# The last three steps of both S5 recurrences: one product pass and one and three quarters of a GLU pass put ahead of the transposes

## The chip, the cores and the metric

One core of a Trainium2 chip runs the whole program. The core has a matrix engine (PE, with a weight loader of its own, PEld), a vector engine (DVE), a scalar engine (ACT), a general engine (POOL) and a queue for transfers (SP). Each works through its own list of instructions in order, and they wait for one another by semaphores. The metric is the device time of one execution in microseconds (us), the median of three runs.

## The reference

A trunk of four layers over 512 positions of 1024 channels: S5, gated linear attention, differential attention, S5, each followed by a SwiGLU feed-forward layer, with a final norm. The change lies in the two S5 layers:

```python
def s5_mixer(h, lam_re, lam_im, log_dt, b_re, b_im, c_re, c_im, d_skip, w_glu):
    ...
        bu_re = jnp.einsum('bcgh,gph->bcgp', u_c, bb_re)
        ...
        _, _, s_re, s_im = lax.associative_scan(_cdiag_combine, (a_re, a_im, bu_re, bu_im), axis=1)
        ...
        y = jnp.einsum('bcgp,ghp->bcgh', s_re, cr) - jnp.einsum('bcgp,ghp->bcgh', s_im, ci)
        return (s_re[:, -1], s_im[:, -1]), y
    ...
    y = y + d_skip.astype(f32) * h.astype(f32)
    z = jax.nn.gelu(y).astype(h.dtype)
    a, b = jnp.split(z @ w_glu, 2, axis=-1)
    return a * jax.nn.sigmoid(b)
```

A bank of complex one-pole recurrences is driven by the input `u`, read out into `y`, passed through a GELU to `z`, and `z` goes through a gated linear unit (GLU) of 1024 x 2048 weights.

## The kernel before

Both S5 layers run `s5_pipe`. The 1024 channels are cut into eight blocks of 128, and a loop of ten steps, `kk` = 0 to 9, keeps several blocks in flight. "Block 5" below is the sixth block, and `glu(5)` its GLU products. What happens to a block:

- `up` (line 1447, PE) transposes its input; `products` (line 1468, PE) multiplies it by the input operators into two PSUM banks `V`;
- `states` (lines 1473 to 1478, DVE) rotates `V`, `scan` (line 1482, DVE) runs the recurrence, `turn` (lines 1491 and 1495, DVE) rotates back into the four parts `prods`;
- `outputs` (lines 1502 and 1504, PE) multiplies input and `prods` by the output operators into the bank `y`, and ACT makes the GELU of it (line 1506) into `z`;
- `turned` (line 1516, PE) transposes `z` in four pieces into the bank `zp`; ACT copies `zp` to `zT` rounded for the matrix engine (line 1517), and `rest` (line 1520, DVE) makes what the rounding left, so that `zT` has a high and a low part;
- `glu` (lines 396 to 398, PE) adds the block's share to four accumulators `acc`, one for each tile of 128 positions, three products of 512 columns each (high times high, high times low, low times high): 12 matmuls for a block.

Weights of the GLU are loaded for two blocks at once, and split by ACT (line 368, high) and DVE (line 376, low) at the start of an even step. Blocks 6 and 7 share a pair, which is split in step 8.

A step issues, in this order on PE: `outputs(kk - 1)`, `up(kk + 2)`, `turned(kk - 1)`, `products(kk + 1)`, `glu(kk - 2)`. In step 8 there are no products left, and `glu(6)` stands ahead of `turned(7)`. The order of all five engines in this loop is the order of the code: it is written out by hand (`hand_all`), and no scheduler moves anything in it.

Around the loop the two layers differ. The first one (about 28 to 156 us of the trace) builds its operators while it runs: in its step 6 the operators of block 7 are transposed (line 1270, PE) and copied by ACT (line 1293) into `inm`, which `products(7)` reads, and the skip-and-decay operator of blocks 6 and 7 goes through DRAM and back (lines 1246 to 1261) before `outputs(6)` can read it. The second one (about 1760 to 1852 us) loads its operators from DRAM, where an earlier part of the program put them (SP, lines 1856 and 1861).

Right behind the loop the same four accumulators are emptied by ACT (line 1904), the other three quarters of the GLU follow on PE, and then the feed-forward layer.

Of the kernel before, what the change touches and what calls it, by code (L numbers as in the profile page):

```python
# [24 lines left out]
NT = SEQ // P  # L25
# [263 lines left out]
class Trunk:  # L289
# [1132 lines left out]
    def s5_pipe(self, L, hu, zT, natural, room, get, before=None, hooks=None, steps=None, left=None):  # L1422
# [19 lines left out]
        def up_first(kk):  # L1442
            ps = self.acc("up")[:].rearrange("p (b m) -> p b m", b=4) if left and kk in (1, 2, 3) else self.tp("up")[:]
            ups[kk] = ps
            for b in range(4):
                g0 = 8 * kk + 2 * b
                nc.tensor.transpose(
                    ps[:, b], hu[:, g0 : g0 + 2].rearrange("p g t c -> p (g t c)"), self.ident[:]
                )

        def up(kk):
            if kk not in ups:
                up_first(kk)
            ps, o = ups[kk], room[kk % 4]
            if left and kk < 4:
                v.tensor_tensor(
                    o.rearrange("p (b m) -> p b m", b=4), ps, left.Rt.unsqueeze(1).broadcast_to([P, 4, P]), op=ALU.mult
                )
            else:
                nc.scalar.copy(o, ps.rearrange("p b m -> p (b m)"))  # L1460

        def products(kk):

            U, inm = room[kk % 4], get(kk, "in")
            V[kk] = [self.sbank("V"), self.sbank("V")]
            for z in range(2):
                for b in range(4):
                    mm(V[kk][z][:, bs(b)], inm[:, z, bs(b)], U[:, bs(b)], start=True, stop=True)  # L1468

        def states(kk):  # L1470

            cs, m = get(kk, "cs"), hold[kk % 2][0]
            v.tensor_tensor(m[:, 0], V[kk][0][:], cs[:, 0], op=ALU.mult)
            v.tensor_tensor(m[:, 3], V[kk][0][:], cs[:, 1], op=ALU.mult)
            v.tensor_tensor(m[:, 1], V[kk][1][:], cs[:, 1], op=ALU.mult)
            v.tensor_tensor(m[:, 2], V[kk][1][:], cs[:, 0], op=ALU.mult)
            v.tensor_tensor(m[:, 0], m[:, 0], m[:, 1], op=ALU.add)
            v.tensor_tensor(m[:, 2], m[:, 2], m[:, 3], op=ALU.subtract)

        def scan(kk, z):  # L1480
            m = hold[kk % 2][0]
            v.tensor_tensor_scan(m[:, 1 + 2 * z], get(kk, "r4"), m[:, 2 * z], 0.0, op0=ALU.mult, op1=ALU.add)

        def turn(kk, k):

            cs = get(kk, "cs")
            m, q = hold[kk % 2]
            sh = lambda x: x.rearrange("p (b m) -> p b m", m=P)[:, :, : P - 1]
            a, b = ((1, 0), (3, 1), (3, 0), (1, 1))[k]
            if k == 1:  # L1490
                v.scalar_tensor_tensor(
                    q[:, k, :, 1:], sh(m[:, a]), -1.0, sh(cs[:, b]), op0=ALU.mult, op1=ALU.mult
                )
            else:
                v.tensor_tensor(q[:, k, :, 1:], sh(m[:, a]), sh(cs[:, b]), op=ALU.mult)

        def outputs(kk):

            U, om, mop, q = room[kk % 4], get(kk, "out"), get(kk, "map"), hold[kk % 2][1]
            yb = self.tp("y")  # L1500
            for b in range(4):
                mm(yb[:, b], U[:, bs(b)], mop[:, bs(b)], start=True, stop=False)
                for j in range(4):
                    mm(yb[:, b], q[:, j, b], om[:, j // 2, bs(b)], start=False, stop=j == 3)  # L1504
            z = room[4 + kk % 2].rearrange("p (t n) -> p t n", t=4)
            nc.scalar.activation(
                z.rearrange("p t (g h) -> p g t h", h=16),
                yb[:].rearrange("p b (g t h) -> p (b g) t h", t=4, h=16), AF.Gelu_apprx_tanh,
            )

        def turned(kk):
            z = room[4 + kk % 2].rearrange("p (t n) -> p t n", t=4)
            zps[kk] = zp = self.tp("zp")[:].rearrange("p a b -> p (a b)")
            order = "p (m t) -> p t m" if natural else "p (t m) -> p t m"
            for t in range(4):
                nc.tensor.transpose(zp.rearrange(order, t=4)[:, t], z[:, t], self.ident[:])
            self.last_turned = nc.scalar.copy(zT[:, 0, kk], zp)

        def rest(kk):
            v.tensor_tensor(zT[:, 1, kk], zps[kk], zT[:, 0, kk].bitcast(F32), op=ALU.subtract)  # L1520

        def glu(kk):
            if not accs:
                accs.extend(self.acc() for _ in range(NT))
            hl = hls[kk // 2]
            for t in range(NT):
                ts = slice(t * P, (t + 1) * P)
                self.mm3(
                    accs[t][:], zT[:, 0, kk, ts], zT[:, 1, kk, ts], hl[:, 0, kk % 2], hl[:, 1, kk % 2],
                    kk == 0, kk == KT - 1,  # L1530
                )

        if hooks:
            hook = lambda name, kk: hooks[name](kk) if name in hooks else None
            late = hooks.get("late", ())
            self.hand_all()
            if left:
                for kk in range(4):
                    up_first(kk)
            before(up, products)  # L1540
            for kk in range(10):
                if kk % 2 == 0 and kk:
                    hls[kk // 2 - 1] = self.high(stage[kk // 2 - 1], 2, 512)
                hook("first", kk)
                if kk < 8:
                    states(kk)
                if kk == 7:
                    rest(5)
                if kk - 1 in late:
                    scan(kk, 0)  # L1550
                    scan(kk, 1)
                    rest(kk - 2)
                if kk % 2 == 0 and kk:
                    self.low(hls[kk // 2 - 1], stage[kk // 2 - 1])
                hook("behind states", kk)
                if 1 <= kk < 9 and kk not in late:
                    outputs(kk - 1)
                hook("operators", kk)
                if kk + 2 < 8:
                    up(kk + 2)  # L1560
                hook("ahead of zp", kk)
                if kk == 8:
                    glu(6)
                if 1 <= kk < 9 and kk not in late:
                    turned(kk - 1)
                if kk + 1 < 8:
                    products(kk + 1)
                hook("behind products", kk)
                if kk < 8:
                    if kk - 1 not in late:  # L1570
                        scan(kk, 0)
                        scan(kk, 1)
                    hook("behind scans", kk)
                    for k in range(4):
                        turn(kk, k)
                hook("beside", kk)
                if kk in late:
                    outputs(kk - 1)
                    turned(kk - 1)
                elif 1 <= kk < 9 and kk != 6:  # L1580
                    rest(kk - 1)
                if kk % 2 == 0 and kk < 8:
                    stage[kk // 2] = self.staged(self.wb_src(wg, kk, D), 2, 512)
                if kk >= 2 and kk != 8:
                    glu(kk - 2)
                hook("last", kk)
            self.hand()
            return accs
# [5 lines left out]
        for kk in range(11):  # L1594
            if kk < 8:
                products(kk)
                states(kk)
            if 1 <= kk < 9:
                scan(kk - 1, 0)
                turn(kk - 1, 0)  # L1600
                scan(kk - 1, 1)
                for k in (1, 2, 3):
                    turn(kk - 1, k)
            if kk + 1 < 8:
                up(kk + 1)
            if steps:
                steps(kk)
            if 2 <= kk < 10:
                outputs(kk - 2)
            if kk % 2 == 0 and kk < 8:  # L1610
                stage[kk // 2] = self.staged(self.wb_src(wg, kk, D), 2, 512)
            if kk % 2 and 3 <= kk:
                j = (kk - 3) // 2
                hls[j] = self.halves(stage[j], 2, 512)
            if 2 <= kk < 10:
                turned(kk - 2)
                rest(kk - 2)
            if kk >= 3:
                glu(kk - 3)
# [944 lines left out]
```

## Time and profile before

| what | us |
|---|---|
| three runs | 2268.05, 2264.08, 2266.39 (median 2266.39) |
| the profiled execution, its own time | 2265.08 |
| its span, first to last instruction | 2263.3 |
| PE busy | 2200.7 |
| DVE busy | 1561.8 |
| ACT busy | 1121.4 |
| mean granted clock of PE | 0.992 |

The profiled execution's own time is 1.78 us above its span and 1.31 us under the median of the runs. A row of a timeline below has the start in us, the duration in us, the engine, the line, the operation, output and inputs, shapes and the number of merged instructions; at its end, in brackets, stands how long the engine was idle before it and who ended that. A matmul of full-precision operands has two entries in the trace (a `products` pass is 16 entries, an `outputs` pass 40), and one of the GLU has one. The end of a matmul is modelled, and the next one starts before it.

### The profile page before, as it was taken

How to read it: one execution, taken by the hardware profiler on the slowest of the kernel's cores; microseconds unless marked ns; L12 is line 12 of the kernel's file. 1: busy time of each engine (PE TensorE's matmuls, PEld its weight loads, DVE VectorE, ACT ScalarE, POOL GpSimd, SP SyncE). 2: the span in 40 equal slices, each digit the busy share in tenths (PEclk: the TensorE clock that was granted, in tenths of full speed). 3: DMA queues.
4: the chain of work that ended last, by engine and by line, in shares of the span. 5: the costliest groups of instructions: out<-in, count | busy, mean ns of one | idle time of the engine just before them, and what ended most of it. 6: DMA issues, size and time to landing. Idle time of an engine off the chain costs nothing.

```text
span 2263.3 us, 37243 instructions
## 1 busy us (share of the span) xinstructions
PE 2200.7 (97%) x14847; PEld 1952.7 (86%) x14847; DVE 1561.8 (69%) x2424; ACT 1121.4 (50%) x1878; POOL 281.2 (12%) x392
## 2 busy tenths in 40 slices
PE   5999999999999999999999999999999899999998
PEld 4878979889777799998988887999998788989997
DVE  9963977776625479777754675977766964967675
ACT  6534645453453456555535676744544224635343
POOL 1000141522000011101002131111000100101000
PEclk8999999999999999999999999999999999999999
DMA  4257475663422557766336366985641546676632
GB/s 88 52 154 188 115 192 159 172 188 90 124 75 65 142 143 185 191 162 172 99 127 142 91 147 161 237 219 134 175 101 39 147 144 166 169 186 158 168 75 75
DMA packets 296039, 317.83 MB, mean 140 GB/s; under 512 B 72285, under 2 KB 235417, under 8 KB 295482
## 3 DMA queue, kind: packets, MB, share of 16 engines
q1 hardware_dynamic: 233626, 234.23, 34.4%
q0 software_dynamic: 62240, 81.22, 19.3%
q8 instruction: 117, 1.92, 0.4%
q14 instruction: 56, 0.46, 0.1%
HBM read 283.54 MB, written 16.65 MB: 133 GB/s over the span
## 4 chain that ended last, share of the span: by engine, by line
PE 83%; DVE 8%; ACT 4%; issue 2%; DMA 1%; SPq 1%; POOL 0%; ACTq 0%; DVEq 0%; POOLq 0%
PE a L541 18%; PE acc L396 14%; PE acc L398 13%; PE acc L397 13%; PE c L541 8%; PE d L541 4%; PE y L1504 2%; DVE whl L376 2%; ACT whl L368 1%; PE V L1468 1%; PE op L2366 1%; PE s L2332 1%; PE tp L123 1%; DVE halves L229 1%; ACT halves L211 1%
## 5 line engine op out<-in xcount | busy, mean ns | idle before, releaser
L376 DVE TENSOR_TENSOR whl<-wst,whl 128x1024 fp32r<-128x1024 f32 x272 | 331.2, 1222 | 260.7 <-ACT whl L368 260.2
L368 ACT CAST whl<-wst 128x1024 fp32r<-128x1024 f32 x272 | 283.9, 1050 | 310.3 <-PE acc L398 227.2
L541 PE MATMUL a<-side,whl 128*128 128x256 f32 x3168 | 382.3, 277 | 4.0 <-DVE whl L376 3.6
L541 PEld LDWEIGHTS a<-side,whl 128*128 128x128 f32 x3168 | 369.0, 188 | 6.8 <-DVE whl L376 5.4
L396 PE MATMUL acc<-whl,act 128*128 128x512 f32 x680 | 268.9, 396 | 1.9 <-DVE x L524 1.9
L397 PE MATMUL acc<-whl,act 128*128 128x512 f32 x680 | 265.3, 390 | 0.0
L398 PE MATMUL acc<-whl,act 128*128 128x512 f32 x680 | 265.3, 390 | 0.0
L541 PE MATMUL c<-side,whl 128*128 128x256 f32 x2112 | 254.3, 277 | 1.2 <-DVE whl L376 1.2
L541 PEld LDWEIGHTS c<-side,whl 128*128 128x128 f32 x2112 | 246.7, 188 | 2.0 <-DVE whl L376 2.0
L376 DVE TENSOR_TENSOR whl<-slot,whl 128x1024 fp32r<-128x1024 f32 x107 | 130.4, 1221 | 70.4 <-ACT whl L368 70.4
L396 PEld LDWEIGHTS acc<-whl,act 128*128 128x128 f32 x680 | 127.6, 188 | 31.3 <-issue 2.7
L368 ACT CAST whl<-slot 128x1024 fp32r<-128x1024 f32 x107 | 112.2, 1053 | 83.0 <-PE acc L398 34.9
L398 PEld LDWEIGHTS acc<-whl,act 128*128 128x128 f32 x680 | 127.7, 188 | 27.0
L397 PEld LDWEIGHTS acc<-whl,act 128*128 128x128 f32 x680 | 127.7, 188 | 24.7
L396 PE MATMUL acc<-whl,hT 128*128 128x512 f32 x352 | 142.6, 405 | 0.0
L398 PE MATMUL acc<-whl,hT 128*128 128x512 f32 x352 | 138.1, 392 | 0.0
L397 PE MATMUL acc<-whl,hT 128*128 128x512 f32 x352 | 137.8, 392 | 0.0
L541 PE MATMUL a<-sides,whl 128*128 128x256 f32 x1056 | 134.5, 283 | 0.0
L541 PEld LDWEIGHTS a<-sides,whl 128*128 128x128 f32 x1056 | 129.7, 191 | 1.2
L541 PE MATMUL d<-sides,whl 128*128 128x256 f32 x1056 | 126.5, 276 | 1.0 <-ACT whl L368 1.0
L541 PEld LDWEIGHTS d<-sides,whl 128*128 128x128 f32 x1056 | 122.8, 188 | 1.2 <-ACT whl L368 1.2
L680 ACT CAST act<-r 128x512 fp32r<-128x512 f32 (+1 forms) x110 | 66.4, 646 | 114.9 <-DVE r L659 107.6
(478 smaller groups left out, 3909.9 us busy)
## 6 DMA issues: line engine op xcount, KB each, us to landing
wst<-in_ffn_w_gate_up_dram SPq DMA_DIRECT2D x88, 512.0 KB, 4.7
wst<-in_ffn_w_down_dram SPq DMA_DIRECT2D x88, 512.0 KB, 4.4
slot<-in_ffn_w_gate_up_dram SPq DMA_DIRECT2D x71, 512.0 KB, 5.3
wst<-in_ffn_w_gate_up_dram POOLq DMA_DIRECT2D x44, 512.0 KB, 6.3
halves<-in_ffn_w_gate_up_dram SPq DMA_DIRECT2D x43, 512.0 KB, 5.4
wst<-in_s_w_glu_dram SPq DMA_DIRECT2D x32, 512.0 KB, 4.7
wst<-in_gla_w_in_dram SPq DMA_DIRECT2D x24, 512.0 KB, 3.7
wst<-in_diff_w_qkv_dram SPq DMA_DIRECT2D x24, 512.0 KB, 4.4
```

Of the source, the lines that this page charges most:

```text
L123: tr.nc.tensor.transpose(p[:, j], h[:, j * P : (j + 1) * P], tr.ident[:])
L211: self.tr.nc.scalar.mul(self.F[t // 2, d][:, j, (t % 2) * P : (t % 2 + 1) * P], p[:, j], self.gcol[:, 4 * d + j : 4 * d + j + 1])
L229: v.tensor_tensor(s, s, y, op=op)
L368: self.last["high"] = self.nc.scalar.copy(hl[:, 0], w[:])
L376: self.last["low"] = self.nc.vector.tensor_tensor(hl[:, 1], w[:], hl[:, 0].bitcast(F32), op=ALU.subtract)
L396: mm(out, lh, rh, start=first, stop=False)
L397: mm(out, lh, rl, start=False, stop=False)
L398: self.last["mm"] = mm(out, ll, rh, start=False, stop=last)
L541: mm(o, hl[:, x, k, c], side[y][:, k], start=first and not (j or k or n), stop=k == 3 and n == 2, skip_group_check=True,)
L680: self.last["act high"] = nc.scalar.copy(dst[:, 0, j], src[:, j])
L1468: mm(V[kk][z][:, bs(b)], inm[:, z, bs(b)], U[:, bs(b)], start=True, stop=True)
L1504: mm(yb[:, b], q[:, j, b], om[:, j // 2, bs(b)], start=False, stop=j == 3)
```

## The change

Nothing is added and nothing removed; three passes of PE change places, in both layers:

```diff
-        def glu(kk):
+        def glu(kk, tiles=range(NT)):
...
-            for t in range(NT):
+            for t in tiles:
...
+                if kk == 6:
+                    products(7)
+                if kk == 7:
+                    glu(5)
                 if kk == 8:
-                    glu(6)
+                    glu(6, range(3))
                 if 1 <= kk < 9 and kk not in late:
                     turned(kk - 1)
-                if kk + 1 < 8:
+                if kk == 8:
+                    glu(6, range(3, NT))
+                if kk + 1 < 7:
                     products(kk + 1)
...
-                if kk >= 2 and kk != 8:
+                if kk >= 2 and kk not in (7, 8):
                     glu(kk - 2)
```

The lists of DVE, ACT, POOL and SP stay as they are. On PE, step 6 of the second layer (`V` are the products of block 7, `zp` the transposes of block 5, `acc` the GLU products of block 4):

```order
 L1502 MATMUL y<-out_16976,room_16969 128x128
 L1504 MATMUL y<-out_16976,prods 128x128 x4
+L1468 MATMUL V<-room_16969,in_16971 128x128 x8
 L1516 MATMUL zp<-ident,room_16969 128x128 x4
-L1468 MATMUL V<-room_16969,in_16971 128x128 x8
 L396 MATMUL acc<-whl,zT 128x512
 L397 MATMUL acc<-whl,zT 128x512
```

The products now follow the outputs directly, and the transposes come behind them. The first layer has the same change of places, with `xps` (line 1270) between the outputs and the products.

On PE, step 7 of the first layer, with the waits (`gain` is the room in which `z` of block 6 lies; before, the four transposes stood ahead of the twelve GLU products):

```order
 L1502 MATMUL y<-scr_97,room_352 128x128
 L1504 MATMUL y<-scr_97,prods 128x128 x4
-L1516 MATMUL zp<-ident,gain 128x128 [waits DVE_49,Activation_49]
+L396 MATMUL acc<-whl,zT 128x512 [waits Activation_49]
+L397 MATMUL acc<-whl,zT 128x512
+L398 MATMUL acc<-whl,zT 128x512 [waits DVE_49]
```

The GLU products of block 5 now follow the outputs of block 6, and the transposes of block 6 come behind all twelve of them.

On PE, step 8 of the first layer (the transposes of block 7 among the GLU products of block 6):

```order
 L397 MATMUL acc<-whl,zT 128x512
 L398 MATMUL acc<-whl,zT 128x512
-L396 MATMUL acc<-whl,zT 128x512
-L397 MATMUL acc<-whl,zT 128x512
-L398 MATMUL acc<-whl,zT 128x512
 L1516 MATMUL zp<-ident,z_353 128x128 x4
+L396 MATMUL acc<-whl,zT 128x512
+L397 MATMUL acc<-whl,zT 128x512
+L398 MATMUL acc<-whl,zT 128x512
```

The three products of the last tile of block 6 moved from ahead of the transposes to behind them, in front of the products of block 7.

## The prediction

> **What bounds the kernel now.** The page first: which engine is full, and which chain ends last.
>
> ```profile
> PE 2200.7 (97%) x14847; PEld 1952.7 (86%) x14847; DVE 1561.8 (69%) x2424; ACT 1121.4 (50%) x1878; POOL 281.2 (12%) x392
> PE 83%; DVE 8%; ACT 4%; issue 2%; DMA 1%; SPq 1%; POOL 0%; ACTq 0%; DVEq 0%; POOLq 0%
> ```
>
> The matrix engine (PE) is busy for 97% of the span and makes 83% of the chain. So a reordering of PE's list can only win PE's idle time, and the view of waits says what ended it:
>
> ```profile
> PE zp L1516 <- ACT room L1506: 3.6, 7, 1.0
> PE zp L1516 <- ACT gain L1506: 1.4, 2, 0.7
> PE acc L396 <- ACT zT L1517: 1.3, 2, 0.7
> ```
>
> In each step the transposes (`zp`) wait for ACT's GELU of outputs that PE has only just finished. In step 8 the GLU products wait for ACT's copy of the transposes. The change touches two of the nine waits of the first two rows in the second layer, one in the first layer, and both of the last row. The timeline of PE shows them in the second layer:
>
> ```profile
> 1814.32 1.06 PE L1504 MATMUL y<-out,prods 128*128 128x128 f32 x8
> 1815.22 0.60 PE L1447 MATMUL up<-ident,hu 128*128 128x128 f32 x4
> ...
> 1824.74 1.06 PE L1504 MATMUL y<-out,prods 128*128 128x128 f32 x8
> 1826.83 0.66 PE L1516 MATMUL zp<-ident,room 128*128 128x128 f32 x4 [1.03 <-ACT room L1506]
> 1827.32 1.95 PE L1468 MATMUL V<-room,in 128*128 128x128 f32 x16
> 1829.03 0.48 PE L396 MATMUL acc<-whl,zT 128*128 128x512 f32 x1
> ...
> 1831.85 0.38 PE L1502 MATMUL y<-out,room 128*128 128x128 f32 x2
> ...
> 1835.42 1.06 PE L1504 MATMUL y<-out,prods 128*128 128x128 f32 x8
> 1837.23 0.66 PE L1516 MATMUL zp<-ident,room 128*128 128x128 f32 x4 [0.75 <-ACT room L1506]
> 1837.64 0.48 PE L396 MATMUL acc<-whl,zT 128*128 128x512 f32 x1
> ...
> 1840.47 0.38 PE L1502 MATMUL y<-out,room 128*128 128x128 f32 x2
> ...
> 1844.04 1.06 PE L1504 MATMUL y<-out,prods 128*128 128x128 f32 x8
> 1844.85 0.48 PE L396 MATMUL acc<-whl,zT 128*128 128x512 f32 x1
> ...
> 1847.70 0.60 PE L1516 MATMUL zp<-ident,room 128*128 128x128 f32 x4
> 1848.97 0.50 PE L396 MATMUL acc<-whl,zT 128*128 128x512 f32 x1 [0.67 <-ACT zT L1517]
> ...
> 1849.70 0.50 PE L398 MATMUL acc<-whl,zT 128*128 128x512 f32 x1
> ```
>
> Step 6 runs from the third row, step 7 from 1831.85, step 8 from 1840.47. I count by starts. The last group of an outputs pass takes 0.90 until full-precision work that waits for nothing (1814.32 to 1815.22), and 0.81 until a GLU product (1844.04 to 1844.85). Transposes take 0.49 until full-precision work (1826.83 to 1827.32) and 0.41 until a GLU product (1837.23 to 1837.64). Twelve GLU products take 2.85 (1844.85 to 1847.70), a pass of `products` 1.71 until a GLU product (1827.32 to 1829.03), and 1.80 until transposes, by the same 0.09 that the outputs show.
>
> **The change part by part.** The same instructions run in another order, so no time is added but what a change of kind costs between neighbours, and that is in these intervals. No DMA is issued by any moved pass, and the lists of SP and POOL stay.
>
> *Step 6, second layer.* Products may start at 1824.74 + 0.90 = 1825.64, transposes at 1827.44, GLU products of block 4 at 1827.85, where they start at 1829.03: **1.18 us won**. Are the operands there? The operators of block 7 are issued on SP here:
>
> ```profile
> 1817.98 1.28 SPq L1856 DMA_DIRECT2D in<-in  x2
> ...
> in<-in SPq DMA_DIRECT2D x4, 128.0 KB, 3.1
> ```
>
> They land about 3.1 behind the second issue, 1819.26 + 3.1 = 1822.4, 3 us early. The GELU that the transposes wait for ends at 1826.77 (next fence), 0.67 ahead of them; with the products gone from that place it would cost what it costs now.
>
> ```profile
> 1826.17 0.60 ACT L1506 ACTIVATE room<-y 128x512 f32<-128x512 f32 x1 [3.71 <-PE y L1504]
> ...
> 1837.92 0.59 ACT L1517 CAST zT<-zp 128x512 fp32r<-128x512 f32 x1 [0.74 <-PE zp L1516]
> 1838.40 1.06 ACT L368 CAST whl<-wst 128x1024 fp32r<-128x1024 f32 x1
> ```
>
> *Step 7, second layer.* The GLU products of block 5 follow the outputs at once: 1835.42 + 0.81 = 1836.23, then 2.85, then transposes 0.49, so the next outputs start at 1839.57 in place of 1840.47: **0.90 won**. The GELU is covered by 2.85 of products. These need the low part of block 5, which DVE makes at 1832.02 (below); they now start at 1836.23 - 1.18 = 1835.05, over 2 us later.
>
> *Step 8, second layer.* Nine products instead of twelve stand ahead of the transposes, which so start 3 x 0.23 = 0.69 earlier. Behind them the first product of block 7 comes 1.27 after their start (1847.70 to 1848.97), the third 2.00 after (1849.70), held by ACT's copy and DVE's low part. The last tile fits in between: 0.41 + 0.77 = 1.18. **0.69 won**; a fourth of the pass is used, and 0.09 of the wait is left.
>
> *First layer.* The same steps:
>
> ```profile
> 130.36 2.05 PE L1468 MATMUL V<-room,inm 128*128 128x128 f32 x16 [0.75 <-ACT inm L1293]
> 132.16 0.48 PE L396 MATMUL acc<-whl,zT 128*128 128x512 f32 x1
> ...
> 136.17 0.46 PE L1502 MATMUL y<-scr,room 128*128 128x128 f32 x2 [0.99 <-DMA scr<-rd]
> ...
> 139.82 1.06 PE L1504 MATMUL y<-scr,prods 128*128 128x128 f32 x8
> 141.62 0.66 PE L1516 MATMUL zp<-ident,gain 128*128 128x128 f32 x4 [0.75 <-ACT gain L1506]
> ...
> 144.86 0.39 PE L1502 MATMUL y<-scr,room 128*128 128x128 f32 x2
> ```
>
> In step 6 the products wait for ACT's copy of their operators, so they cannot start before 130.36. The transposes, which filled part of that wait, come behind and push the GLU products 0.41 back. That is a loss, and it is hidden: the next outputs wait until 136.17 for an operator coming back from DRAM, 0.99 idle. Without that cover it costs 0.41. In step 7: 139.82 + 0.81 + 2.85 + 0.49 = 143.97 for 144.86, **0.89 won**. Step 8 has the same intervals as the second layer: **0.69**.
>
> *What comes later in its place.* The transposes of block 6 start later (second layer: 1835.05 + 2.85 = 1837.90, for 1837.23), so do ACT's copy and its weight cast behind it, and DVE's rest and low part behind those:
>
> ```profile
> 1832.02 0.68 DVE L1520 TENSOR_TENSOR zT<-zp,zT 128x512 fp32r<-128x512 f32 x1
> ...
> 1836.04 1.28 DVE L1495 TENSOR_TENSOR prods<-mods,cs 128x508 f32<-128x508 f32 x2
> ...
> 1839.49 1.22 DVE L376 TENSOR_TENSOR whl<-wst,whl 128x1024 fp32r<-128x1024 f32 x1 [0.26 <-ACT whl L368]
> ```
>
> The low part ends 3.48 after the transposes start (1837.23 to 1840.71), so at 1841.4. The GLU products of block 6 need it at 1839.57 - 1.18 + 4.38 = 1842.8 (an outputs pass is 4.38, 1840.47 to 1844.85). The margin is 1.4, and the same in the first layer. The parts that the last outputs read are done at 1837.32, and these start at 1838.39, 1.07 later. DVE's rest of block 5 (1832.02) needs a copy that now ends near 1828.7; behind it in DVE's list stand the scans of block 7, so 3.3 of margin matter there.
>
> *The sum.* 1.18 + 0.90 + 0.69 + 0.89 + 0.69 = **4.35 us**. From both sides: if only the idle column can be won, with 0.09 off for each change of kind, it is 0.94 + 2 x 0.66 + 2 x 0.58 = 3.4; if every interval goes by the shorter of the two measured, 1.27 + 2 x 0.98 + 2 x 0.69 = 4.6. I take starts, since they were seen without a wait between the same kinds of work.
>
> A page of the Trainium skill bears on this choice: "Perfetto Trace Analysis", the section on the tensor engine's instruction, says that a matmul's end in a trace is computed from its size and not observed. By that the idle column is computed too, and the sum would be 4.35 and not 3.4. The trace agrees: the bar at 1814.32 is 1.06 long, and the next work starts after 0.90.
>
> **Does it reach the end?** Behind each loop PE is full:
>
> ```profile
> 153.00:225.00 72.00, 71.61 (x326) 58.79 (x327) 29.59 (x33) 31.90 (x63) 5.10 (x4) 1.00 0.70 190
> 1849.00:1920.00 71.00, 70.98 (x323) 58.29 (x324) 29.05 (x32) 30.90 (x61) 5.18 (x4) 1.00 0.66 178
> ```
>
> (length, then busy time of PE, of its weight loader, DVE, ACT and POOL, clock, DMA share, GB/s.) Whatever starts earlier there ends earlier. The second layer's 2.77 has no transfer on the chain behind it. The first layer's 1.58 passes some:
>
> ```profile
> 571.78 5.09 DMA wst<-in_gla_w_in_dram
> ...
> 1017.94 3.79 DMA wst<-in_ffn_w_down_dram
> ...
> 1356.39 8.70 DMA wst<-in_diff_w_o_dram
> ```
>
> Each is issued when a buffer comes free, so it moves along.
>
> **The rivals.** Around what? The profiled execution took 2265.08, of which 2263.3 is span; the three runs have a median of 2266.39, and all four executions a mean of 2265.90. I subtract from that mean, since one run says little at this size. 0.2% (4.5 us) is about what a measurement of this kernel can tell from no change.
>
> - *Forecast: all five gaps close.* 2265.90 - 4.35 = **2261.6**, 0.21% under the median shown. Chance 0.74.
> - *Only the idle column is won*, 3.4 us: 2262.5. For it, waits on semaphores now stand between passes that ran together; against it, the intervals above. 0.07.
> - *Step 7 doesn't do what it says:* the moved GLU products wait on ACT, and if that wait counts up to the GELU of block 6, nothing is won there. Then 1.18 + 2 x 0.69 = 2.6 is left: 2263.3. Against it, the copy that they need (block 5) is ahead of that GELU in ACT's list. 0.06.
> - *The first layer's gain is lost at the transfers above:* a load that started earlier and took longer would eat 1.58, so 2.77 is left: 2263.1. The spread of those rows, 3.79 to 8.70, speaks for it; that they begin with a buffer's release, against. 0.08.
> - *Slower: the later transposes hold up the weights' low part.* In step 8 the GLU products would wait for DVE (line 376), as ACT casts behind its copy and DVE subtracts behind its rest. Each us beyond the margin of 1.4 costs one in each layer, so it outweighs 4.35 from 3.6 us late on. With the pair's load late by 6 us on top, it costs 2 x 4.6: 2265.90 - 4.35 + 9.2 = 2270.8. For it, the longest load above is 8.70; against it, ACT started its cast right behind the copy, so the load had landed. 0.05.
>
> **How the numbers follow.** The forecast lies only 0.3 us beyond the edge of 0.2% (2261.86). The medians spread by about 1.2, from runs 4.0 apart, so a bit more than six in ten of its 0.74 fall beyond the edge, 0.46, and 0.28 within. The other three gains add 0.02 beyond and 0.19 within. Together: faster 0.48, same 0.47, slower 0.05. The range holds the gains from 1.7 to 6.7 around the mean: 2259.2 to 2264.2; it takes in all cases but the last, and the bounds 3.4 and 4.6.
>
> **What would show it right or wrong.** In the changed trace, no idle time ahead of `zp` in steps 6 and 7 of the second layer and in step 7 of the first. From the last group of the outputs of block 5 to the first GLU product of block 7, PE needs 2.77 less in the second layer (now 1824.74 to 1848.97, 24.23). In the first layer step 6 starts its products at 130.36 again, relative to the loop, and the outputs behind still wait for DRAM, by 0.6 instead of 0.99. The three products of the last tile stand between the last transposes and block 7, with about 0.1 idle. It would be wrong if GLU products wait in step 7 for ACT or in step 8 for DVE, if the outputs of block 7 wait for `prods`, or if the gaps close and the stretch from 1849 to the end grows by as much.

## The result and the profile after

The changed kernel takes 2263.69 us in the median of 22 runs (2259.45 to 2267.82), the kernel before 2267.09 us in 22 runs (2264.08 to 2271.07). The ratio is 0.9983 with a 95% interval from 0.9977 to 0.9989: 3.9 us less, between 2.5 and 5.2. That is a gain, and at 0.17% it is a little inside the 0.2% that was set as the edge. The profiled execution took 2260.07 us, with a span of 2258.4.

In the view of PE's waits of the changed kernel, the two rows on the transposes have lost two waits and one, and the row of GLU products waiting for ACT's copy (1.3 us before) is gone:

```profile
PE zp L1516 <- ACT room L1506: 1.9, 5, 0.7
...
PE zp L1516 <- ACT gain L1506: 0.7, 1, 0.7
```

PE's timeline in the second layer of the changed kernel, steps 6 to 8:

```profile
1822.16 1.06 PE L1504 MATMUL y<-out,prods 128*128 128x128 f32 x8
1823.06 1.95 PE L1468 MATMUL V<-room,in 128*128 128x128 f32 x16
1824.84 0.60 PE L1516 MATMUL zp<-ident,room 128*128 128x128 f32 x4
1825.20 0.48 PE L396 MATMUL acc<-whl,zT 128*128 128x512 f32 x1
...
1831.60 1.06 PE L1504 MATMUL y<-out,prods 128*128 128x128 f32 x8
1832.41 0.48 PE L396 MATMUL acc<-whl,zT 128*128 128x512 f32 x1
...
1835.26 0.60 PE L1516 MATMUL zp<-ident,room 128*128 128x128 f32 x4
1835.69 0.39 PE L1502 MATMUL y<-out,room 128*128 128x128 f32 x2
...
1839.27 1.06 PE L1504 MATMUL y<-out,prods 128*128 128x128 f32 x8
...
1842.24 0.60 PE L1516 MATMUL zp<-ident,room 128*128 128x128 f32 x4
1842.60 0.47 PE L396 MATMUL acc<-whl,zT 128*128 128x512 f32 x1
...
1843.15 0.40 PE L398 MATMUL acc<-whl,zT 128*128 128x512 f32 x1
1843.52 0.50 PE L396 MATMUL acc<-whl,zT 128*128 128x512 f32 x1
1843.86 0.40 PE L397 MATMUL acc<-whl,zT 128*128 128x512 f32 x1
1844.25 0.50 PE L398 MATMUL acc<-whl,zT 128*128 128x512 f32 x1
```

No row has a bracket, and in steps 6 and 7 the starts show no wait either. In step 8 they show a small one: the last product of block 6 and the three of block 7 start 0.37, 0.34 and 0.39 apart (1843.15 to 1844.25), where products that wait for nothing start 0.23 apart, so 0.41 us of waiting is left. The products of step 6 follow the outputs by 0.90, as 1823.06 - 1822.16 shows. From the last group of the outputs of block 5 to the first GLU product of block 7 (1843.52) it is 21.36 us, for 24.23 before: 2.87 less, where 2.77 was worked out. The same view in the first layer:

```profile
130.38 2.05 PE L1468 MATMUL V<-room,inm 128*128 128x128 f32 x16 [1.34 <-ACT inm L1293]
132.27 0.60 PE L1516 MATMUL zp<-ident,z 128*128 128x128 f32 x4
...
136.44 0.46 PE L1502 MATMUL y<-scr,room 128*128 128x128 f32 x2 [0.82 <-DMA scr<-rd]
...
140.08 1.06 PE L1504 MATMUL y<-scr,prods 128*128 128x128 f32 x8
140.90 0.47 PE L396 MATMUL acc<-whl,zT 128*128 128x512 f32 x1
...
143.75 0.60 PE L1516 MATMUL zp<-ident,gain 128*128 128x128 f32 x4
...
152.01 0.50 PE L396 MATMUL acc<-whl,zT 128*128 128x512 f32 x1
```

The products of step 6 start where they did (130.38), after a longer wait, and the outputs behind them still wait for the operator from DRAM. From the last group of the outputs of block 6 (140.08) to block 7's first GLU product it is 11.93 us, for 13.55 before (139.82 to 153.37): 1.62 less, where 1.58 was worked out.

So the loops won 4.49 us in these two executions. The rest of the difference of 4.9 between the spans lies outside the two stretches: the outputs of block 6 started 0.27 later, the program between the two stretches took 1.22 less, and what follows them took 0.55 more. The experiments and the last section take up the 0.27 and the 1.22. The 0.55 is of this one profile: from block 7's first GLU product to the end it has 414.9 us, the ten other profiles of this study between 414.0 and 414.5, whether the second layer was changed or not. Its cause is open.

### The profile page after: what moved, and what is told of

Its sections match the earlier page's. It is cut to its first block, busy times and chain, and to the rows that moved or that the text cites. A ratio compares the mean times of both kernels' runs of the same rounds, so it can differ in the third digit from the quotient of the medians.

```text
span 2258.4 us, 37240 instructions
## 1 busy us (share of the span) xinstructions
PE 2198.9 (97%) x14847; PEld 1951.9 (86%) x14847; DVE 1561.8 (69%) x2424; ACT 1122.5 (50%) x1878; POOL 281.6 (12%) x392
## 4 chain that ended last, share of the span: by engine, by line
PE 81%; DVE 9%; ACT 4%; issue 2%; DMA 2%; SPq 0%; POOL 0%; DVEq 0%; ACTq 0%; POOLq 0%
PE a L541 18%; PE acc L396 13%; PE acc L398 13%; PE acc L397 13%; PE c L541 8%; PE d L541 4%; PE y L1504 2%; DVE whl L376 2%; ACT whl L368 1%; PE V L1468 1%; PE op L2372 1%; PE s L2338 1%; PE tp L123 1%; DVE halves L229 1%; ACT halves L211 1%
```

## The experiments

**Each step alone.** Three kernels, each with one of the three moves. Step 6 alone:

```diff
+                if kk == 6:
+                    products(7)
...
-                if kk + 1 < 8:
+                if kk + 1 < 7:
                     products(kk + 1)
```

> Only the products of block 7 are put ahead of the transposes of block 5; steps 7 and 8 run as before. Read in the second layer from the last group of the outputs of block 5 to the first GLU product of block 7 (24.23 us before, 21.36 with the whole change). Theory, the gap in step 6 closes by itself: about 1.2 us less, 23.0. Rival, the gap only moves on to the next transposes: 24.2. In the first layer, from the last group of the outputs of block 5 to the first of block 6 (10.02 before): theory, the 0.41 lost there lies under the trip through DRAM, 10.0 within what that trip varies (0.3); rival, it is paid, 10.4, with no wait for the DRAM trip left.

PE's timeline in the second layer of this kernel, from the last group of the outputs of block 5 to the first GLU product of block 7:

```profile
1824.78 1.06 PE L1504 MATMUL y<-out,prods 128*128 128x128 f32 x8
1825.67 1.95 PE L1468 MATMUL V<-room,in 128*128 128x128 f32 x16
1827.46 0.60 PE L1516 MATMUL zp<-ident,room 128*128 128x128 f32 x4
...
1836.01 0.66 PE L1516 MATMUL zp<-ident,room 128*128 128x128 f32 x4 [0.75 <-ACT room L1506]
...
1847.76 0.50 PE L396 MATMUL acc<-whl,zT 128*128 128x512 f32 x1 [0.68 <-ACT zT L1517]
```

22.98 us, as expected, with the two other gaps as they were: the gap closes by itself and moves nowhere. In the first layer it is 10.26 us from the last group of the outputs of block 5 (126.13) to the first of block 6 (136.39), with 0.82 us of waiting for the DRAM trip left. The rival wanted 10.4 and no wait. But 10.26 is above the 10.02 of before, so the first layer was looked at once more, below. One execution of this kernel took 2263.76 us, beside 2265.09 of the kernel before.

Step 7 alone:

```diff
+                if kk == 7:
+                    glu(5)
...
-                if kk >= 2 and kk != 8:
+                if kk >= 2 and kk not in (7, 8):
                     glu(kk - 2)
```

> Only the GLU products of block 5 are put ahead of the transposes of block 6. Theory, each layer wins 0.90 us: the second layer's stretch 23.3 for 24.23, and in the first layer from the last group of the outputs of block 6 to the first GLU product of block 7 12.65 for 13.55. Rival, the moved products wait for the GELU of block 6: both stretches as before.

23.30 us in the second layer (1826.96 to 1850.26) and 12.59 in the first (141.71 to 154.30): 0.93 and 0.96 won. The moved products don't wait for the GELU of block 6; that rival has fallen. One execution took 2266.36 us, 1.27 more than the 2265.09 before, although its loops won 1.9: one execution tells nothing of changes this small.

Step 8 alone:

```diff
-                    glu(6)
+                    glu(6, range(3))
                 if 1 <= kk < 9 and kk not in late:
                     turned(kk - 1)
+                if kk == 8:
+                    glu(6, range(3, NT))
```

> Only the last tile of the GLU products of block 6 is put behind the transposes of block 7. Theory, 0.69 us in each layer, three products of 0.23: 23.54 for 24.23 and 12.86 for 13.55, with about 0.1 idle ahead of the first GLU product of block 7. Rival, splitting the pass costs a change of kind that eats a part: 0.5 or less.

23.55 us (1825.54 to 1849.09) and 12.88 (140.38 to 153.26): 0.68 and 0.67 won, three products of 0.23, and the split costs nothing. One execution took 2265.15 us. (Three quarters of this GLU pass stood ahead of the transposes before, too; what the change moves in step 8 is the last quarter, and it moves behind them.)

The three alone add up to 1.25 + 0.93 + 0.68 = 2.86 in the second layer, where the whole change wins 2.87: the steps don't touch one another.

**Step 6 of the first layer in the old order**, everything else changed:

```diff
-                if kk == 6:
+                if kk == 6 and left:
                     products(7)
...
-                if kk + 1 < 7:
+                if kk + 1 < (7 if left else 8):
                     products(kk + 1)
```

> The whole change but for step 6 of the first layer, which keeps the old order. Theory, nothing is lost or won by it: from the last group of the outputs of block 5 to the first of block 6 10.0 us within 0.3, the wait for the DRAM trip back at 1.0 from 0.8, and the GLU products of block 4 0.4 earlier. Rival, the new order there delays the outputs of block 6: they start 0.3 to 0.4 earlier in this kernel than with the whole change.

9.81 us (130.03 to 139.84) with a wait of 0.79 us for the DRAM trip. One execution took 2264.71 us. Beside the 10.27 of the whole change (126.17 to 136.44) the 9.81 is the rival's number. But the wait that is left contradicts its mechanism, and so do the other profiles: what varies is the trip itself. It ends with eight scattering DMA issues on SP, and their time, from the rows of line 1261 on SP in each profile, goes with the stretch:

| profile | order in step 6 | the eight issues, us | outputs to outputs, us |
|---|---|---|---|
| before | old | 4.62 | 10.02 |
| step 7 alone | old | 4.49 | 9.80 |
| step 8 alone | old | 4.37 | 9.90 |
| old order kept here | old | 4.35 | 9.81 |
| whole change | new | 4.86 | 10.27 |
| step 6 alone | new | 4.84 | 10.26 |
| two tiles (below) | new | 4.37 | 9.80 |
| products first in all steps (below) | new | 4.56 | 9.96 |
| the same with the wait filled (below) | new | 4.62 | 10.03 |
| transposes repeated, first layer (below) | new | 4.54 | 9.97 |
| transposes repeated, second layer (below) | new | 4.74 | 10.25 |

The two tiles have the new order, the short trip and the short stretch. There the cover is nearly used up, as PE's timeline says:

```profile
136.64 0.46 PE L1502 MATMUL y<-scr,room 128*128 128x128 f32 x2 [0.34 <-issue]
```

The row puts this gap down to `issue`, where the other ten profiles name the transfer. But in all eleven these outputs start 1.86 to 2.00 us behind the end of the eight issues, and here it is 1.89 (the issues end at 134.75): it is the trip that they follow. So by itself the new order does not hold these outputs up: in every profile a wait for the trip was left, 0.34 us at the least. What stays open is whether it makes the trip longer. The stretch has a mean of 10.08 us in the seven profiles of the new order and of 9.88 in the four of the old one, 0.2 apart where single profiles of one order are up to 0.47 apart. No moved pass issues a DMA, and no mechanism for it was found or tried.

**Does time won in the loops reach the end?** The sums are too small to be read in the whole time, so a larger known time was added at the same places: in step 8 the four transposes of block 7 are repeated, in one layer at a time.

```diff
-            for t in range(4):
+            for t in [0, 1, 2, 3] * (21 if kk == 7 and not left else 1):
                 nc.tensor.transpose(zp.rearrange(order, t=4)[:, t], z[:, t], self.ident[:])
```

> The whole change, and in step 8 of the first layer the four transposes of block 7 are made 21 times into the same bank in place of once: 80 more transposes of about 0.11 us each, 8.8 us more on the matrix engine there, with the same result. It asks whether time in the first layer's loop reaches the end. Theory, what is behind it moves along: 8.8 us more than the whole change, about 2272.5 in the median, 1.0022 of the kernel before. Rival, the loads behind it take a part up (the first layer's gain of 1.6 would then be lost in part too): 3 to 6 us more than the whole change.

Measured: 1.0026 of the kernel before, interval 1.0015 to 1.0036 (median 2271.68 us). In PE's timeline the repeated transposes stand as one row:

```profile
151.14 9.33 PE L1516 MATMUL zp<-ident,z 128*128 128x128 f32 x84
```

From the last group of the outputs of block 7 to the third GLU product of block 7 this kernel takes 13.72 us (148.16 to 161.88), the whole change 4.99 (147.75 to 152.74): 8.73 us were added. Whole times differ by 1.0026 - 0.9983, that is 9.7 us, and with both intervals by 7.0 to 12.5. The 8.73 lies within, the rival's 3 to 6 does not: time added in the first layer's loop moves everything behind it.

For time that is won there, the piece between the layers tells more: from block 7's first GLU product in the first layer to the second layer's first `up` it would be longer by what is lost of the gain. Seven profiles have both gains of the first layer, and a mean of 1601.01 us there; the other four, with one of these gains or none, have 1601.02. Single profiles lie between 1599.76 and 1602.68, so that a loss of the whole 1.6 would show, and a loss of some tenths would not.

> The same 80 transposes in step 8 of the second layer only. Both theories expect 8.8 us more than the whole change, 1.0022 of the kernel before, since no load stands on the chain behind the second layer; less than 7 would say that the end is held by something else.

Measured: 1.0033, interval 1.0020 to 1.0045 (median 2274.03 us); 8.73 us were added here too (1843.84 to 1857.55, for 1839.27 to 1844.25). The difference to the whole change is 11.3 us, between 8.2 and 14.5, which holds the whole 8.73. So a delay of PE reaches the end from both places.

**Two tiles ahead and two behind** in step 8:

```diff
-                    glu(6, range(3))
+                    glu(6, range(2))
...
-                    glu(6, range(3, NT))
+                    glu(6, range(2, NT))
```

> The whole change, but in step 8 two tiles of the GLU products of block 6 stand ahead of the transposes of block 7 and two behind, in place of three and one. Theory, what is left of the wait there is the DVE's low part, 2.0 us after the transposes start; two tiles cover it: from the last group of the outputs of block 7 to the third GLU product of block 7 0.4 us less than with the whole change in each layer. The GELU of block 7 is done in time, 0.9 us after the outputs against 1.5 of products. Whole time about 0.8 us less, too little to tell in the median. Rival, the transposes wait for that GELU: no gain or a loss of up to 0.5.

From the last group of the outputs of block 7 to its third GLU product: 4.58 us in both layers (1839.68 to 1844.26, and 147.97 to 152.55), for 4.98 and 4.99 with three tiles. So 0.4 us in each, and PE's timeline of this kernel shows no wait:

```profile
1841.97 0.60 PE L1516 MATMUL zp<-ident,room 128*128 128x128 f32 x4
1842.32 0.48 PE L396 MATMUL acc<-whl,zT 128*128 128x512 f32 x1
...
1843.80 0.40 PE L396 MATMUL acc<-whl,zT 128*128 128x512 f32 x1
1844.03 0.39 PE L397 MATMUL acc<-whl,zT 128*128 128x512 f32 x1
1844.26 0.40 PE L398 MATMUL acc<-whl,zT 128*128 128x512 f32 x1
```

The products of block 7 (1843.80 on) come at the 0.23 of products that wait for nothing, where with three tiles 0.41 was lost, the end of it to DVE's low part (done at 1844.19 in that profile, the third product at 1844.25). The whole time, 0.9987 with an interval from 0.9979 to 0.9995 (median 2263.36 us), can't be told from that of the change.

**The products first in all steps of the second layer**, with two tiles:

```diff
-                if kk == 6:
-                    products(7)
+                if kk == 6 or left and 1 <= kk < 6:
+                    products(kk + 1)
...
-                if kk + 1 < 7:
+                if kk + 1 < 7 and not (left and kk):
                     products(kk + 1)
```

> As with two tiles ahead and two behind, and in the second layer the products go ahead of the transposes in the steps 1 to 5 too, where the transposes wait 0.69, 0.25, 0.31, 0.31 and 0.31 us. Theory, each of these gaps closes with the 0.09 of its change of kind: 2.3 us less in the second layer, with two tiles 3.0 less than the whole change, a ratio of about 0.997 to the kernel before. Rival, the vector engine, busy without a break in these steps, becomes the bound: the gaps turn into waits for prods and 1 us or less is won.

Measured: 0.9968 of the kernel before, interval 0.9955 to 0.9980 (median 2259.76 us in 5 runs). All waits of the transposes for the GELU in the second layer are gone; the rows on transposes that are left are all of the first layer:

```profile
PE zp L1516 <- ACT Q L1196: 1.0, 2, 0.5
...
PE zp L1516 <- ACT gain L1506: 0.7, 1, 0.7
...
PE zp L1516 <- ACT inm L1293: 0.4, 1, 0.4
```

From the outputs in step 2 to the third GLU product of block 7 it takes 65.10 us (1778.24 to 1843.34), with two tiles alone 66.79 (1777.47 to 1844.26): 1.69 us won in steps 2 to 5, where 0.25 + 3 x 0.31 + 4 x 0.09 = 1.54 was expected. In step 1, from the last group of the outputs to the outputs of step 2, it takes 3.12 (1775.12 to 1778.24) for 4.02 (1773.45 to 1777.47): 0.90 won for 0.78. The vector engine does not become the bound; PE does not wait for it in steps 2 to 8, and its wait for `prods` ahead of step 1's outputs, 2.85 us, was 3.18 with two tiles alone. This version is faster than the kernel before. From the change it differs by 0.15%, with an uncertainty of about the same size.

**The wait ahead of the second layer, filled.** The profiles above show falls of the granted clock at the start of the second layer's loop (last section). This kernel has the products first in all steps, as the last one, and ten matmuls more in the wait ahead of that loop:

```diff
+            for n in range(fill):
+                g0 = 8 * kk + 2 * (n % 4)
+                mm(ps[:, n % 4], hu[:, g0 : g0 + 2].rearrange("p g t c -> p (g t c)"), self.ident[:], start=True, stop=True)
```

> The kernel with two tiles and the products first in all steps of the second layer, and ten matmuls more (2.1 us, into a bank that is written again behind them) in the 2.57 us in which the matrix engine waits ahead of the second layer's loop. It asks whether the granted clock, which in the profiles falls to 0.66 to 0.92 in the 20 us behind that wait, falls because of the idle time. Theory, it does, and the filled wait keeps the clock at 1.00 there: 2 to 5 us less than without the ten, about 0.995 of the kernel before, and a smaller spread. Rival, the clock falls because of what runs there (short full-precision matmuls with waits between them): the same dips, the same time, 0.997.

Measured: 0.9962, interval 0.9948 to 0.9975 (median 2259.56 us): not to be told from 0.9968. The windows of 4 us show what it did (length, busy time of PE, of its weight loader, DVE, ACT and POOL, granted clock, DMA share, GB/s). Without the ten:

```profile
1756.00:1760.00 4.00, 1.68 (x7) 1.52 (x8) 2.04 (x3) 2.44 (x5) 3.26 (x5) 0.71 1.05 267
1760.00:1764.00 4.00, 4.00 (x20) 3.90 (x19) 2.85 (x5) 2.07 (x3) 0.11 (x1) 0.50 1.09 200
1764.00:1768.00 4.00, 1.56 (x12) 1.36 (x10) 4.00 (x6) 0.00 (x0) 0.00 (x0) 0.93 0.79 194
1768.00:1772.00 4.00, 3.59 (x14) 3.30 (x15) 4.00 (x8) 0.00 (x0) 0.00 (x0) 0.50 0.47 173
```

and with them:

```profile
1760.00:1764.00 4.00, 2.35 (x17) 2.00 (x17) 2.67 (x5) 3.62 (x7) 2.23 (x4) 1.00 1.11 241
1764.00:1768.00 4.00, 2.72 (x18) 2.23 (x18) 4.00 (x7) 0.90 (x1) 0.00 (x0) 1.00 1.06 178
1768.00:1772.00 4.00, 2.10 (x8) 1.72 (x9) 4.00 (x7) 0.00 (x0) 0.00 (x0) 0.79 0.93 275
```

The first fall is gone: the clock stays at 1.00 until 1768, and falls only behind the next waits (0.90 for a transfer, 2.04 for `prods`). In each of the ten profiles without the ten matmuls it falls between 1756 and 1768, in the lowest window of 4 us to between 0.50 and 0.78. So the first fall hangs on that wait, as far as one filled profile shows it. That the waits behind it make the next fall is what the order of the rows suggests; it was not tried.

From the first `up` of the layer to the third GLU product of block 7 it takes 88.95 us (1755.52 to 1844.47), for 90.62 without the ten (1752.72 to 1843.34): 1.67 won in this pair of profiles, under the 2 to 5 expected. Even that is no size to rely on. From the first `up` to the `up` of step 2 this kernel takes 28.55 us and the one without the ten 29.99, but the nine other profiles 29.62 to 30.75, of which the moved products of step 1 would save 0.90: by these the filling is worth 0.2 to 1.3 us. The runs spread over 2.7 us for 4.3 without the ten, which five runs of each don't settle.

## Why the prediction was right

- **The gaps in steps 6 and 7**, 1.18 and 0.90 in the second layer and 0.89 in the first: each alone gave 1.25, 0.93 and 0.96. Counting by starts was right and the bound from the idle column (0.94 and 0.66) too low by about 0.3. The error left is 0.03 to 0.07 on each term: transposes that wait for nothing take 0.36 until a GLU product (1824.84 to 1825.20) and 0.43 until full-precision work (1835.26 to 1835.69), where 0.41 and 0.49 were read off transposes that had waited.
- **Step 8**, 0.69 in each layer: 0.68 and 0.67. A wait was left, as was said, but only its first part was counted, the 0.09 ahead of the first product of block 7; it was 0.41 over the three, and two tiles take it.
- **Step 6 of the first layer**, a loss of 0.41 under the DRAM trip: hidden, as said. The wait expected to be left was 0.6; it was 0.82 with a longer trip and 0.34 with a short one.
- **What comes later in its place**: DVE's timeline in the second layer of the changed kernel has both.

```profile
1833.30 1.28 DVE L1495 TENSOR_TENSOR prods<-mods,cs 128x508 f32<-128x508 f32 x2
...
1837.46 1.23 DVE L376 TENSOR_TENSOR whl<-wst,whl 128x1024 fp32r<-128x1024 f32 x1 [0.25 <-ACT whl L368]
```

The low part of the weights ends at 1838.69, 1.39 ahead of its use at 1840.08, where 1.4 was worked out. The parts that the last outputs read end at 1834.58, and these start 1.11 later, at 1835.69, where 1.07 was worked out. The slower rival had no place to begin in this profile.

- **It reaches the end**: shown for both layers for the added 8.73 us, and for the first layer's gain by the piece between the layers, which is not longer with it. So the rival that loses the whole 1.58 there has fallen; the timed runs alone, 2.5 to 5.2, would have left its 2.77 open.
- **The size**: 4.35 was worked out, the profiles have 4.49 in the loops, and the timed runs 3.9 (2.5 to 5.2). The 2261.6 is 2.1 below the median of 2263.69. Of that, 1.2 is the base, the mean of four executions (2265.90) where 22 have a median of 2267.09, and 0.9 is the gain by the medians, 3.4 for 4.35. The median lies 0.5 inside the upper end of the range, so that the number came out inside owes something to luck: a base from four executions could have been further off. The gains read in the loops owe nothing to it.
- **The edge**: more of the forecast's chance lay beyond 0.2% than within. The measured 0.17% is within, and its interval reaches to 0.23%: nothing in the mechanism decides on which side it falls.

## What to carry to other kernels

On an engine that is full, a wait for another engine's answer to its own last pass is closed by putting ahead of it any pass that is ready and as long as the answer takes; what must be checked is which later work hangs on the step that was pushed back, with its margin in us. Read the gain from start to start, against the same pair of passes at a place without a wait, since the idle column of a matrix engine is short by the modelled end. A change worth 0.2% is settled by such local stretches and not by single executions: step 7 alone won 1.9 us in the loops and its one execution was slower than the kernel before.

## What the runs showed of the hardware that was not expected

The granted clock of PE falls for some us at three places of the program, and not by the same amount each time: between 40 and 60 us (0.56 and 0.59 by windows of 10 us, in the kernel before and in the changed one), at 650 us and at the start of the second layer. In the profile of the kernel before:

```profile
650.00:660.00 10.00, 10.00 (x55) 8.69 (x54) 1.23 (x1) 1.35 (x3) 0.00 (x0) 0.83 0.29 92
1760.00:1770.00 10.00, 7.09 (x38) 6.39 (x38) 9.14 (x15) 3.68 (x6) 1.08 (x3) 0.75 0.97 201
```

and in that of the changed kernel, where nothing around 650 us was changed:

```profile
650.00:660.00 10.00, 10.00 (x62) 8.86 (x61) 1.23 (x1) 1.66 (x3) 0.00 (x0) 1.00 0.18 53
1760.00:1770.00 10.00, 6.63 (x34) 5.48 (x34) 9.58 (x16) 1.14 (x1) 0.07 (x1) 0.84 0.89 204
```

At 650 us the profile shows no wait behind the fall: PE counts as busy for the whole of both windows. What runs there is a pass of 32 matmuls with two columns each, and then products of 512 columns. In the kernel before, some of these come 0.43 apart:

```profile
651.54 3.63 PE L2005 MATMUL dps<-ind,la 128*128 128x2 f32 x32
...
657.66 0.63 PE L397 MATMUL acc<-whl,hT 128*128 128x512 f32 x1
658.09 0.63 PE L398 MATMUL acc<-whl,hT 128*128 128x512 f32 x1
```

and in the changed kernel 0.23 apart:

```profile
650.33 3.63 PE L2011 MATMUL dps<-ind,la 128*128 128x2 f32 x32
...
656.44 0.39 PE L398 MATMUL acc<-whl,hT 128*128 128x512 f32 x1
656.67 0.39 PE L396 MATMUL acc<-whl,hT 128*128 128x512 f32 x1
```

From the start of that pass to the twentieth product behind it, the kernel before takes 9.52 us (651.54 to 661.06) and the changed one 7.92 (650.33 to 658.25). This one fall cost 1.60 us, more than the 1.22 that the program between the loops took less in the profile of the change. The ten other profiles of this study all had a fall at 650 or 660 us, to between 0.66 and 0.84 by windows of 10 us; why one execution was spared is open.

The runs of the changed kernel go with the mean clock: its 5 runs with 0.991 took 2263.08 to 2267.82 us, its 5 with 0.994 or 0.995 took 2259.52 to 2260.40. The kernel before does not show this: four of its runs with 0.995 took 2265.34 to 2268.63, around its medians in the same sessions (2265.74 and 2267.42). The runs of the changed kernel spread over 8 us, twice what the change is worth.

The Trainium skill, on the page "TensorE: Matmul & The Clock Gate" in the section "Part 1: The HAM clock gate", says that the gate opens with sustained work of the matrix engine and closes when it idles, by windows of some 3.4 us that run freely. The filled wait agrees: with 2.57 and 1.13 us of waiting nearly in a row the clock fell, with the first of them filled it stayed at 1.00. The fall at 650 us does not fit as simply, since by the profile PE does not idle there. That windows run freely would explain falls of different depth at the same place; no run here shows the windows themselves.
